# Two blocks' values per run, attention transposes two steps behind, norm factors in the weights, and VectorE making every low weight part

## The chip, the cores and the metric

The kernel runs on one core of a Trainium2 chip. Its engines are TensorE (PE, with its weight loads shown as PEld), VectorE (DVE), ScalarE (ACT), GpSimd (POOL) and the queue of SyncE (SP) that issues most transfers. The metric is device time in microseconds (us) for one launch. Before the change it is 1147.07 us, the median of three runs from 1146.75 to 1149.39 us.

## The reference

One encoder layer over 1024 tokens of width 1024, with 16 learned meta tokens in front, all in float32:

```
u = rmsnorm(h, norm_g)                       # h: 16 meta tokens + 1024 tokens
z = u @ w_in                                 # one projection, split by columns
gq gk gv r_f r_b g_gate  nq nk nv n_gate = split(z)

# group A: gated linear attention, 4 heads, both directions, chunked scan
o_gla = rmsnorm(o_f + o_b, gla_out_norm_g) * silu(g_gate)

# group B: neighbourhood attention, 16 heads of 64, on a 16 x 64 grid
qn, kn = rmsnorm(nq, q_norm_g), rmsnorm(nk, k_norm_g)
s   = qn . kn / 8 + rpb (8 x 16 window)  ++  qn . km / 8 + meta_bias
o_na = softmax(s) . (v window ++ v meta) * silu(n_gate)

out = h + concat(o_gla, o_na) @ w_out        # the 16 meta tokens are dropped
```

Here `rmsnorm(x, g)` is x times 1/sqrt(mean(x^2) + 1e-6) times g. The factor `norm_g` multiplies each of the 1024 input columns of the projection, so it can as well multiply the rows of `w_in`: (x * g) @ w equals x @ (g * w). The factor 1/sqrt of a token is applied after the projection, in both kernels.

## The kernel before

**Split products.** A float32 product is made of three TensorE matmuls. Each operand is split into a high part in TensorE's rounded float format (`wh`, `uh`) and the remainder (`wl`, `ul`); `mm3` (L414 to L416) multiplies high by high, high by low and low by high into one PSUM bank. These dense matmuls of the projection are nearly all of TensorE's work. The token side, `uh` and `ul`, is made once, at the start, per block of 128 tokens (`u_part` for the first two blocks, `u_split` for the other six). The weight side comes in pieces of 128 rows by up to 512 columns: `piece_dma` loads one into `raw`, and `piece_split` makes `wh` and `wl` from it when a slot of nine comes free (`release`, `pump`). Three pairings of engines are used there: ACT for `wh` with POOL for `wl` (63 pieces), DVE for both (24 pieces), and ACT with DVE (63 pieces, once the linear attention has begun). The tables `SPLIT_ACT` and `NA1_ACT` choose between the first two.

**Two interleaved programs.** `Sched` records the program in an order written out at build time. A filler (`fill_na`, later `fill_gla`) gives the dense matmuls in small steps; a main generator gives the attention. `S.run` lets the main generator place its own TensorE work and, between (`gap`, `to`), as much filler as it asks for; `need` runs filler until a named result is due. `S.defer(ns, fn)` places other engines' work a number of estimated nanoseconds later. Every engine then executes its own list strictly in that order and waits on semaphores. So TensorE always has dense work to do, unless an instruction at the head of its list waits.

**Neighbourhood attention, pair by pair.** Eight pairs of heads run through `attn(p)`. Each pair has eight query blocks u (128 queries each). For pair p the projection tiles (`dense_na`) give `nat` (queries and keys) and `vnat` (values); `k_prep` transposes the keys on TensorE (`kmt`, `kt`) into `K1`, `K2`; `q_prep` transposes two blocks of queries (`qt`). A step s does this, on two heads a = 0, 1:

- `transposes` of block s-1: the normalised probabilities P are transposed into the PSUM banks `pp` (L829, 6 matmuls), and copied into `PT` by ACT for a = 0 and DVE for a = 1;
- `softmax(s)`: the scores (`qk`, L767 and L768, into banks `s`), row maximum and bias on DVE (L795), exponential on ACT (L801, L802), and, deferred, `norm` (L815 to L818) on DVE, which divides P by its sum;
- filler for half a step;
- `pv` of block s-1: six matmuls (L848) of `PT` with the values, into one bank `po` whose two halves of 64 rows hold the two heads; the trace has two records for each of these matmuls. After blocks 3 and 7 DVE multiplies `po` into the gate `ng` (L858);
- filler for the other half.

There are 9 steps for 8 blocks: the ninth holds the transposes and values of block 7 alone. Then `attn(p+1)` starts with `need` and `k_prep`. The third chunk of values of blocks 0 and 7 is `kvm`, the 16 meta tokens, the only chunk with 16 rows.

**PSUM.** Eight banks: `pd` 2 (dense), `ps` 2 (scores, and at the start `junk` and `rb`), `pp` 2 (transposes), `po` 1, `pt` 1.

**The start.** `u_rstd` squares a block's rows on ACT, into a bank `junk` that nothing reads, and POOL makes `rs`, the 1/sqrt factor of each token. For the transposed outputs the factors of a block must stand along the free axis, in all partitions (`rbc`): `u_diag` makes a diagonal matrix `dg` on DVE (L376), and `u_spread` multiplies it with a matrix of ones on TensorE (`rb`, L381) and copies the result. The table `START_AT` gives the place of each such step in pair 0's dense work.

**Later.** `wd_prep` (L1018 to L1024) prepares the decay weights, for pairs 2 and 4, 20 us after those pairs' start in the scheduler's count. From about 630 us on the linear attention runs, then the output projection (`pout`), without neighbourhood attention.

## Time and profile before

| | |
|---|---|
| median of three runs | 1147.07 us |
| the profiled execution's own time | 1147.51 us |
| its span, first to last instruction | 1145.7 us |
| TensorE busy | 1122.2 us, 98% |
| VectorE, ScalarE, GpSimd busy | 769.9, 533.5, 300.7 us |
| mean granted TensorE clock | 0.998 |

The profile page gives busy time per engine and per group of instructions; the groups' last column is the idle time of the engine just before them, with what ended it. Matmuls overlap in their pipeline and a "busy" TensorE need not be streaming at its pace: two dense matmuls in a row start a fixed time apart, and whatever one start is later than that is lost, whether or not the page shows it as idle. So the timeline of starts is read here beside the idle column. The stages: start to about 60 us, one pair of heads for each 68 to 69 us until about 541 us, the end of neighbourhood attention and the first linear attention weights to about 630 us, then linear attention and output projection.

### The profile page before, as it was taken

To read this page: it belongs to the slowest core of one execution; us is meant where nothing else is said; L and a number is where in the kernel's file an instruction comes from. 1 tells how busy PE (TensorE), PEld (TensorE's weight loads), DVE (VectorE), ACT (ScalarE), POOL (GpSimd) and SP (SyncE) were. 2 spreads that over 40 slices of the span, in tenths; PEclk is the share of its full clock that TensorE was granted. 3 is DMA by queue.
4 is the path that set the end of the run, shared out by engine and by line. 5 is a ranking of instruction groups with operands and counts; after the bars stand their busy time and mean duration, and the time that the engine had idled before them with its cause. 6 is when DMAs were issued, how large, how long until landed. Compare 5 with 4: busy or idle time off the path is not lost.

```text
span 1145.7 us, 18925 instructions
## 1 busy us (share of the span) xinstructions
PE 1122.2 (98%) x6739; PEld 976.7 (85%) x6739; DVE 769.9 (67%) x1963; ACT 533.5 (47%) x1379; POOL 300.7 (26%) x415
## 2 busy tenths in 40 slices
PE   8899999999999999999999999999999999999998
PEld 7789898888988889898889789889978978888886
DVE  6867777777677776777665775675486578656352
ACT  6756565664655656565454541542343254313120
POOL 4753535336253443634221101001101000000000
PEclk9999999999999999999999999999999999999999
DMA  8720402203030030401223513512612375314132
GB/s 259 225 75 2 128 2 73 63 2 128 1 109 27 10 120 1 128 2 32 76 57 102 165 28 84 153 36 79 170 42 66 93 206 166 120 42 130 50 115 102
DMA packets 74277, 99.34 MB, mean 87 GB/s; under 512 B 6532, under 2 KB 45188, under 8 KB 74184
## 3 DMA queue, kind: packets, MB, share of 16 engines
q1 hardware_dynamic: 69960, 89.76, 26.0%
q0 software_dynamic: 4224, 8.39, 2.5%
q8 instruction: 53, 0.87, 0.3%
q14 instruction: 40, 0.33, 0.1%
HBM read 72.89 MB, written 21.04 MB: 82 GB/s over the span
## 4 chain that ended last, share of the span: by engine, by line
PE 79%; DVE 7%; issue 5%; POOL 3%; ACT 3%; DMA 2%; SPq 0%; POOLq 0%; DVEq 0%; ACTq 0%
PE pn_na L414 6%; PE pn_na L416 5%; PE pn_na L415 5%; PE pout L414 5%; PE pout L416 5%; PE pout L415 5%; PE po L848 3%; PE pp L829 3%; PE pz_gz L414 3%; PE pz_gz L415 3%; PE pz_gz L416 3%; PE pz_gg L414 2%; PE pn_gv L414 2%; PE pz_gg L416 2%; PE pz_gg L415 2%
## 5 line engine op out<-in xcount | busy, mean ns | idle before, releaser
L414 PE MATMUL pn_na<-wh,uh 128*128 128x384 f32 x512 | 179.7, 351 | 1.5 <-ACT wh L257 1.0
L415 PE MATMUL pn_na<-wl,uh 128*128 128x384 f32 x512 | 173.5, 339 | 1.7 <-POOL wl L258 1.4
L416 PE MATMUL pn_na<-wh,ul 128*128 128x384 f32 x512 | 173.0, 338 | 0.1
L212 POOL TENSOR_SCALAR post<-post 128x1 f32<-128x1 f32 x32 | 6.8, 213 | 378.4 <-ACT on L1219 378.4
L414 PEld LDWEIGHTS pn_na<-wh,uh 128*128 128x128 f32 x512 | 96.4, 188 | 10.0 <-issue 7.8
L414 PE MATMUL pout<-wh,oh 128*128 128x512 f32 x256 | 103.3, 404 | 0.2 <-DVE acc L1343 0.2
L416 PE MATMUL pout<-wh,oh 128*128 128x512 f32 x256 | 101.4, 396 | 0.0
L415 PE MATMUL pout<-wl,oh 128*128 128x512 f32 x256 | 101.4, 396 | 0.0
L415 PEld LDWEIGHTS pn_na<-wl,uh 128*128 128x128 f32 x512 | 96.6, 189 | 4.1 <-POOL wl L258 3.0
L416 PEld LDWEIGHTS pn_na<-wh,ul 128*128 128x128 f32 x512 | 96.4, 188 | 0.8 <-DVE ul L361 0.7
L258 POOL TENSOR_TENSOR wl<-raw,wh 128x512 fp32r<-128x512 f32 (+2 forms) x63 | 83.2, 1337 | 45.0 <-PE pn_gv L415 27.7
L1343 DVE TENSOR_TENSOR acc<-acc,pout 128x512 f32<-128x512 f32 x64 | 43.9, 685 | 66.8 <-PE pout L416 66.8
L801 ACT ACTIVATE P<-P,sm 128x384 f32<-128x384 f32 x96 | 58.4, 609 | 56.2 <-DVE sm L798 56.2
L414 PE MATMUL pn_gv<-wh,uh 128*128 128x256 f32 (+1 forms) x256 | 75.3, 294 | 0.0
L416 PE MATMUL pn_gv<-wh,ul 128*128 128x256 f32 (+1 forms) x256 | 72.8, 285 | 0.0
L415 PE MATMUL pn_gv<-wl,uh 128*128 128x256 f32 (+1 forms) x256 | 72.8, 284 | 0.0
L795 DVE CUSTOM_DVE_ANT_0 P<-s,wt 128x416 f32<-128x416 f32 (+1 forms) x128 | 69.6, 544 | 2.3 <-PE s L768 2.2
L213 POOL TENSOR_TENSOR ss<-ss,epsm 128x4 f32<-128x4 f32 x64 | 69.0, 1078 | 5.3
L818 DVE TENSOR_SCALAR P<-P,sm 128x384 f32<-128x384 f32 (+1 forms) x128 | 66.9, 523 | 4.5
L254 ACT ACTIVATE wh<-raw 128x512 fp32r<-128x512 f32 x63 | 39.5, 630 | 48.7 <-PE pz_gz L415 20.4
L835 DVE COPY PT<-pp 128x384 f32<-128x384 f32 (+1 forms) x80 | 36.3, 470 | 33.5 <-PE pp L829 33.0
L416 PEld LDWEIGHTS pout<-wh,oh 128*128 128x128 f32 x256 | 48.3, 189 | 11.6
(361 smaller groups left out, 2969.4 us busy)
## 6 DMA issues: line engine op xcount, KB each, us to landing
raw<-in_w_na_dram SPq DMA_DIRECT2D x56, 256.0 KB, 2.8
v_scr<-gvst SPq DMA_DIRECT2D x64, 128.0 KB, 2.3
raw<-in_w_o_dram SPq DMA_DIRECT2D x32, 256.0 KB, 3.2
oin<-o_scr SPq DMA_DIRECT2D x32, 256.0 KB, 3.1
v<-v_scr POOLq DMA_DIRECT2D x4, 1536.0 KB, 9.4
VM<-vnat SPq DMA_DIRECT2D x8, 512.0 KB, 4.5
o_scr<-ng SPq DMA_DIRECT2D x8, 512.0 KB, 3.5
raw<-in_w_gz_dram SPq DMA_DIRECT2D x16, 256.0 KB, 2.8
```

What stands on the lines that cost most here:

```text
L213: pool.tensor_tensor(dst, dst, epsm[: dst.shape[0], :eng_n], OP.pow)
L254: act.activation(wh[:, :n], r[:, :n], AF.Copy)
L258: pool.tensor_tensor(wl[:, :n], r[:, :n], f32(wh[:, :n]), OP.subtract)
L414: pe.matmul(ps, ah, bh, start=start, stop=False)
L415: pe.matmul(ps, ah, bl, start=False, stop=False)
L416: pe.matmul(ps, al, bh, start=False, stop=stop)
L795: dve.tensor_tensor_reduce(P[:, :n], ps[:, :n], wt[2 * p + a][:, off : off + n], 1.0, -3.0e38, OP.add, OP.max, mx)
L801: act.activation(loc, loc, AF.Exp, bias=mx, accum_out=sm[:, a : a + 1])
L818: dve.tensor_scalar(loc, loc, r, None, OP.mult)
L829: pe.transpose(pp[:w, c * 128 : c * 128 + 128], Ps[a][0][:, c0 : c0 + w], ident)
L835: dve.tensor_copy(t[:w, e0:e1], pp[:w, e0:e1])
L1343: dve.tensor_tensor(a, a, ps, OP.add)
```

## The change

1. **Attention (`attn` becomes `attn_all`).** One generator for all pairs. The transposes of a block now come two steps after its scores instead of one (`wait` holds up to two blocks, `turn` transposes one). Transposed blocks collect in `done`, and `gather` does their value products: at steps 3, 5 and 7, two blocks each time, in one run. Blocks 6 and 7 are finished after the next pair's `need`: a `turn`, 2000 ns of filler, a `turn`, 700 ns, the next pair's `k_prep`, 800 ns, and one `gather` (`TAIL_NS`). The buffers of `P` go from 4 to 6 and of `sm` from 2 to 3. The second load of the values (`vload`) is due by step 3 instead of 1.
2. **Norm factors.** `norm_g` no longer multiplies the tokens: `u_part` copies, `u_split` and `u_meta` lose a DVE multiplication. `piece_split` multiplies each weight row by its factor instead, as the scale of ACT's copy and as the first operation of DVE's.
3. **Weight split.** Every `wh` is made by ACT, every `wl` by DVE; POOL makes none, DVE makes no `wh`. A piece that packs two or four row blocks takes two or four instructions on each engine, since each has its own factor. The output projection's pieces stay as they were.
4. **Start.** `u_rstd` squares in place instead of into a PSUM bank. `u_diag` is gone: `u_spread` uses the column of factors, broadcast along its free axis, as the stationary operand and the identity as the moving one.
5. **Small moves.** The static copies into `K2` and `Q2` go from DVE to ACT, `wd_prep` makes its high part on ACT and reads it directly.

```diff
@@ piece_split
-            if gpool[0] is not None:
+            if key[0] == "o":
                 act.activation(wh[:, :n], r[:, :n], AF.Copy)
                 dve.tensor_tensor(wl[:, :n], r[:, :n], f32(wh[:, :n]), OP.subtract)
-            elif (NA1_ACT[j - 8] if 8 <= j < 16 else SPLIT_ACT[key[0]][j % 4]):
-                act.activation(wh[:, :n], r[:, :n], AF.Copy)
-                pool.tensor_tensor(wl[:, :n], r[:, :n], f32(wh[:, :n]), OP.subtract)
-            else:
-                dve.tensor_copy(wh[:, :n], r[:, :n])
-                dve.tensor_tensor(wl[:, :n], r[:, :n], f32(wh[:, :n]), OP.subtract)
+            for t in range(pack if key[0] != "o" else 0):
+                ts = slice(t * (n // pack), (t + 1) * (n // pack))
+                g = gT[:, pack * i + t : pack * i + t + 1]
+                act.activation(wh[:, ts], r[:, ts], AF.Copy, scale=g)
+                dve.scalar_tensor_tensor(wl[:, ts], r[:, ts], g, f32(wh[:, ts]), OP.mult, OP.subtract)
@@ u_part, u_split
-        g = gT[:, k : k + 1]
-        act.activation(uh[:, k, ts], xk, AF.Copy, scale=g)
-        dve.scalar_tensor_tensor(ul[:, k, ts], xk, g, f32(uh[:, k, ts]), OP.mult, OP.subtract)
+        act.activation(uh[:, k, ts], xk, AF.Copy)
+        dve.tensor_tensor(ul[:, k, ts], xk, f32(uh[:, k, ts]), OP.subtract)
...
-        for ks in halves:
-            dve.tensor_tensor(x3[:, ks], x3[:, ks], gT[:, ks, None].to_broadcast([128, 4, 128]), OP.mult)
@@ u_rstd, u_diag, u_spread
-            junk = ps_tile("ps", f"junk{b}_{i}", 2)
-            act.activation(junk, xr[b][:, 512 * i : 512 * i + 512], AF.Square, accum_out=st[:, i : i + 1])
+            half = xr[b][:, 512 * i : 512 * i + 512]
+            act.activation(half, half, AF.Square, accum_out=st[:, i : i + 1])
...
-    def u_diag(b):
-        dg[b] = nap.tile([128, 128], F32, tag="dg", name=f"dg{b}", bufs=3)
-        dve.tensor_scalar(dg[b], ident, rs[:, b : b + 1], None, OP.mult)
...
-        pe.matmul(ps[:, 0:128], ones, dg[b], start=True, stop=True)
+        pe.matmul(ps[:, 0:128], rs[:, b : b + 1].to_broadcast([128, 128]), ident, start=True, stop=True)
@@ attn becomes attn_all (softmax, transposes and pv are otherwise as before)
-        for s in range(9):
-            PT = None
-            if prev is not None:
-                PT = transposes(*prev)
-                pu = prev[0]
+        def turn():
+            p, u, *rest = wait.pop(0)
+            done.append((p, u, transposes(p, u, *rest)))
+
+        def gather():
+            while done:
+                pv(*done.pop(0))
+
+        for p in range(NPAIR + 1):
+            if p < NPAIR:
+                yield ("need", ("nat", p))
+            if wait:
+                turn()
                 yield ("w", 654)
-            if s < 8:
-                prev = (s, *softmax(s))
+                yield ("gap", TAIL_NS[0])
+                turn()
+                yield ("w", 654)
+                yield ("gap", TAIL_NS[1])
+            if p < NPAIR:
+                yield from k_prep(p)
+            if done:
+                yield ("gap", TAIL_NS[2])
+                gather()
+                yield ("w", 1420)
...
+            yield ("gap", ATTN_NS - (TAIL_NS[2] + 1420.0 if p else 0.0))
...
+            for s in range(8):
+                if len(wait) == 2:
+                    turn()
+                    yield ("w", 654)
+                wait.append((p, s, *softmax(p, s)))
...
-            else:
-                yield ("gap", LAST_NS)
-            if PT is not None:
-                if s == 1:
-                    for m in vload:
-                        m()
-                pv(pu, PT)
-                yield ("w", 710)
+                if s % 2 and s > 1:
+                    if s == 3:
+                        for m in vload:
+                            m()
+                    gather()
+                    yield ("w", 1420)
@@ wd_prep
-        dve.tensor_copy(w[0:98], st[0:98, 0:512])
-        act.activation(st[64:98, 512:1024], f32(w[64:98]), AF.Copy)
-        dve.tensor_tensor(w[64:96], st[64:96, 0:512], st[64:96, 512:1024], OP.subtract)
+        act.activation(w[0:98], st[0:98], AF.Copy)
+        dve.tensor_tensor(w[64:96], st[64:96], f32(w[64:96]), OP.subtract)
```

The number of TensorE instructions is the same; their order is not. The first place is a value product in the middle of pair 1, on TensorE. In the names, `pn` is a dense tile, `PT120` the transposed probabilities of pair 1, block 2, head 0, and `vnat1`, `VM` are its values. Before:

```order
L416 MATMUL pn_na2_3_1962<-wh21_1547,ul_85 128x384
L848 MATMUL po10_1840<-PT120_1970,vnat1_883 64x128
L848 MATMUL po10_1840<-PT121_1976,vnat1_883 64x128
...
L848 MATMUL po10_1840<-PT120_1970,VM_99 64x128
L848 MATMUL po10_1840<-PT121_1976,VM_99 64x128
L414 MATMUL pn_na2_3_1962<-wh22_1573,uh_84 128x384
```

Now, at step 7, blocks 4 and 5 in one run:

```order
L401 MATMUL pn_na2_7_2223<-wh20_1474,ul_85 128x384
L824 MATMUL po14_2286<-PT140_2164,vnat1_838 64x128
L824 MATMUL po14_2286<-PT141_2170,vnat1_838 64x128
...
L824 MATMUL po14_2286<-PT141_2170,VM_99 64x128
L824 MATMUL po14_2286<-PT150_2246,vnat1_838 64x128
...
L824 MATMUL po14_2286<-PT151_2252,VM_99 64x128
L399 MATMUL pn_na2_7_2223<-wh21_1481,uh_84 128x384
```

Twelve matmuls stand where six stood. In the whole list 64 runs of six become 32 runs of twelve. Of the 64, 57 returned to dense work and 7 ran straight into the next pair's `kmt`; all 32 return to dense work.

The second place is the change from pair 1 to pair 2, on TensorE, where `pz` is the dense gate tile. Now:

```order
L805 MATMUL pp160_2377<-ident_76,P160_2176 128x128 x3
L805 MATMUL pp161_2383<-ident_76,P161_2184 128x128 x3
...
L805 MATMUL pp170_2403<-ident_76,P170_2258 128x128 x2
L805 MATMUL pp170_2403<-ident_76,P170_2258 16x128
L805 MATMUL pp171_2410<-ident_76,P171_2265 128x128 x2
L805 MATMUL pp171_2410<-ident_76,P171_2265 16x128
...
L673 MATMUL kmt2_2423<-ident_76,kvm2_1842 128x16
L679 MATMUL kt2_0_2426<-ident_76,nat2_0_1694 128x128
...
L824 MATMUL po14_2286<-PT160_2381,vnat1_838 64x128
L824 MATMUL po14_2286<-PT161_2387,vnat1_838 64x128
```

Before, block 6's transposes stood with block 7's scores, and the values of block 7 came directly ahead of `kmt2`. Now two transposes stand alone, six dense matmuls lie between the second of them and `kmt2`, and the keys' banks `kt` are the two `pp` banks just used. The values of both blocks follow the keys.

The third place is the start, on VectorE, where `x_103` is token block 0 and `wl_179` the fourth weight piece. Before:

```order
L349 SCALAR_TENSOR_TENSOR ul<-x_103,gT,uh 128x128 x4
L260 CAST wh_178<-raw_113 128x384
L261 TENSOR_TENSOR wl_179<-raw_113,wh_178 128x384
L349 SCALAR_TENSOR_TENSOR ul<-x_115,gT,uh 128x128 x3
L349 SCALAR_TENSOR_TENSOR ul<-x_103,gT,uh 128x128
```

Now:

```order
L343 TENSOR_TENSOR ul<-x_103,uh 128x128
L256 SCALAR_TENSOR_TENSOR wl_146<-raw_106,gT,wh_145 128x384
L343 TENSOR_TENSOR ul<-x_103,uh 128x128
L256 SCALAR_TENSOR_TENSOR wl_157<-raw_108,gT,wh_156 128x384
L343 TENSOR_TENSOR ul<-x_103,uh 128x128
L256 SCALAR_TENSOR_TENSOR wl_168<-raw_110,gT,wh_167 128x384
```

VectorE now makes the low part of each weight piece between the low parts of the tokens; the first three used to be GpSimd's.

More of the change, by code (lines that the diff above doesn't have):

```diff
@@ L591, in at @@
                 ("load", x_load), ("split", u_split), ("rows", x_rows), ("rstd", u_rstd),
[L592 removed]
+                ("evac", lambda t: tile_evac(banks.pop(t), t)), ("spread", u_spread),
             ):
@@ new lines, with softmax, norm @@
+    po = {}
+    def softmax(p, u):
+        n = span(u)[1]
+        off = 144 if u == 0 else 0
+        sm = nap.tile([128, 8], F32, tag="sm", name=f"sm{p}{u}", bufs=3)
+        Ps, norms = [], []
+        Q1["rest"]()
+        for a in range(2):
+            ps = qk(p, u, a)
+            P = nap.tile([128, 432], F32, tag="P", name=f"P{p}{u}{a}", bufs=6)
+            mx = sm[:, 4 + a : 5 + a]
+            dve.tensor_tensor_reduce(
+                P[:, :n], ps[:, :n], wt[2 * p + a][:, off : off + n], 1.0, -3.0e38, OP.add, OP.max, mx
+            )
+            dve.tensor_scalar(mx, mx, -1.0, None, OP.mult)
+            if n == 416:
+                loc, met = P.rearrange("p (b t) -> p b t", t=BLK)[:, :, 0:128], P[:, 128:144]
+                act.activation(loc, loc, AF.Exp, bias=mx, accum_out=sm[:, a : a + 1])
+                act.activation(P[:, 295:416:8], met, AF.Exp, bias=mx, accum_out=sm[:, 2 + a : 3 + a])
+            else:
+                loc = P[:, :n]
+                act.activation(loc, loc, AF.Exp, bias=mx, accum_out=sm[:, a : a + 1])
+            Ps.append((P, loc))
+        if u % 2 == SILU_STEP:
+            run_silu()
+        def norm(a):
+            s = sm[:, a : a + 1]
+            r = sm[:, 6 + a : 7 + a]
+            if n == 416:
+                dve.tensor_tensor(s, s, sm[:, 2 + a : 3 + a], OP.add)
+            dve.reciprocal(r, s)
+            loc = Ps[a][1]
+            dve.tensor_scalar(loc, loc, r, None, OP.mult)
+        return Ps, [S.defer(NORM_NS[0], lambda: norm(0)), S.defer(NORM_NS[1], lambda: norm(1))]
@@ new lines, in transposes @@
+    def transposes(p, u, Ps, norm):
+        ch = ((0, 128), (144, 128), (128, 16) if u in (0, 7) else (288, 128))
+        PT = []
+        for a in range(2):
+            norm[a]()
+            pp = ps_tile("pp", f"pp{p}{u}{a}", 2)
+            for c, (c0, w) in enumerate(ch):
+                pe.transpose(pp[:w, c * 128 : c * 128 + 128], Ps[a][0][:, c0 : c0 + w], ident)
+            t = nap.tile([128, 384], F32, tag="PT", name=f"PT{p}{u}{a}", bufs=4)
+            for w, e0, e1 in ((128, 0, 256), (16, 256, 384)) if u in (0, 7) else ((128, 0, 384),):
+                if a == 0:
+                    act.activation(t[:w, e0:e1], pp[:w, e0:e1], AF.Copy)
+                else:
+                    dve.tensor_copy(t[:w, e0:e1], pp[:w, e0:e1])
+            PT.append(t)
+        return PT
@@ new lines, in pv @@
+    def pv(p, u, PT):
+        u4 = u % 4
+        if u4 == 0:
+            po[0] = ps_tile("po", f"po{p}{u}", 1)
+        b0 = span(u)[0]
+        vals = [vnat[p][:, b0], vnat[p][:, b0 + 1], kvm[p][:, 128:256] if u in (0, 7) else VM[:, b0 + 2]]
+        for c, V in enumerate(vals):
+            w = V.shape[0]
+            for a in range(2):
+                pe.matmul(
+                    po[0][64 * a : 64 * a + 64, u4 * 128 : u4 * 128 + 128],
+                    V[:, 64 * a : 64 * a + 64],
+                    PT[a][:w, c * 128 : c * 128 + 128],
+                    start=c == 0, stop=c == 2,
+                )
+        if u4 == 3:
+            finish(gate_rest)
+            g = zt[("ng", p)]
+            gv = g.rearrange("p (r i c) -> p i r c", r=16, i=8, c=8)[:, u - 3 : u + 1]
+            dve.tensor_tensor(gv, po[0].rearrange("p (i r c) -> p i r c", i=4, r=16, c=8), gv, OP.mult)
+            if u == 7:
+                sp.dma_start(o_scr[8 + p], g)
@@ new lines, in attn_all @@
+    def attn_all():
+        wait, done = [], []
+        def turn():
[9 more added lines that the diff above has]
+                turn()
+                yield ("w", 654)
+                yield ("gap", TAIL_NS[0])
[8 more added lines that the diff above has]
+                yield ("w", 1420)
+            if p == NPAIR:
+                break
+            vload = v_load(p)
+            if p in WD_AT:
+                wd_load(WD_AT.index(p))
+                S.defer(WD_NS, lambda d=WD_AT.index(p): wd_prep(d))
+            if p == NPAIR - 2:
+                r_static()
+            yield ("gap", ATTN_NS - (TAIL_NS[2] + 1420.0 if p else 0.0))
+            f0 = S.fill
+            f1 = (p + 1) * (NAT_NS + GATE_NS) + (NAT_NS if p < 7 else GLA_NS - 9000.0)
+            for s in range(8):
[3 more added lines that the diff above has]
+                wait.append((p, s, *softmax(p, s)))
@@ L1356 @@
     S.filler = fill_na()
-    for p in range(NPAIR):
-        if p in WD_AT:
-            wd_load(WD_AT.index(p))
-            S.defer(WD_NS, lambda d=WD_AT.index(p): wd_prep(d))
-        if p == NPAIR - 2:
-            r_static()
-        S.run(attn(p))
+    S.run(attn_all())
     S.until(("gv", 0))
```

111 lines of the change are left out of this document (11 added, 100 removed).

## The prediction

> **What bounds the kernel now.** I read the page first, then the timeline of TensorE's starts.
>
> ```profile
> span 1145.7 us, 18925 instructions
> PE 1122.2 (98%) x6739; PEld 976.7 (85%) x6739; DVE 769.9 (67%) x1963; ACT 533.5 (47%) x1379; POOL 300.7 (26%) x415
> ```
>
> TensorE is busy 98% of the span, and the change removes none of its matmuls. What is left to win is 23.5 us of idle time (1145.7 - 1122.2) and starts that are late without being called idle. The second kind shows in the starts around one value product of pair 3 (start, duration, instruction):
>
> ```profile
> 301.67 0.34 PE L415 MATMUL pn_na<-wl,uh 128*128 128x384 f32 x1
> 301.84 0.34 PE L416 MATMUL pn_na<-wh,ul 128*128 128x384 f32 x1
> 302.11 0.66 PE L848 MATMUL po<-PT,vnat 128*64 128x128 f32 x8
> 302.60 0.39 PE L848 MATMUL po<-PT,VM 128*64 128x128 f32 x4
> 302.91 0.44 PE L414 MATMUL pn_na<-wh,uh 128*128 128x384 f32 x1
> 303.19 0.34 PE L415 MATMUL pn_na<-wl,uh 128*128 128x384 f32 x1
> 303.37 0.34 PE L416 MATMUL pn_na<-wh,ul 128*128 128x384 f32 x1
> ...
> 304.60 0.82 PE L829 MATMUL pp<-ident,P 128*128 128x128 f32 x6
> 305.18 0.44 PE L767 MATMUL s<-K,Q 128*128 128x416 f32 x1
> ```
>
> Dense 384-column matmuls start 0.17 to 0.18 us apart (301.67, 301.84; 303.19, 303.37; I use 0.173). The last before the run is followed after 0.27 (0.10 late). The run's eight records take 0.49, 0.061 each; its last four take 0.31 instead of 0.245 (0.066 late). The first dense one after it is followed after 0.28 (0.107 late). So each run of values costs 0.27 us beside its own work, and there are 64 runs.
>
> **Part 1a, half as many runs.** 57 runs return to dense work, 7 to the next keys:
>
> ```profile
> 128.14 0.40 PE L416 MATMUL pz_na<-uh,wl 128*128 128x512 f32 x1
> 128.47 0.66 PE L848 MATMUL po<-PT,vnat 128*64 128x128 f32 x8
> 129.05 0.43 PE L848 MATMUL po<-PT,kvm 16*64 16x128 f32 x4
> 129.42 0.23 PE L690 MATMUL kmt<-ident,kvm 16*128 16x16 f32 x1
> ```
>
> Here the meta chunk starts 0.58 after the eight (0.09 late, a change to 16 rows), and `kmt` 0.37 after it (0.125 late). The change leaves 32 runs, all to dense work: 25 x 0.27 = 6.8 us go, and 7 x (0.10 + 0.125) = 1.6. Inside a merged run only block 0's meta chunk is followed by a 128-row chunk, so 8 x 0.09 = 0.7 may come, of which some is only moved. Net **-7.9**. Bounds: 0, if lateness belonged to each block rather than to each run, and -8.4. I take -7.9, since it is read at the run's two ends and not between the eight and the four. The transposes cost no entry and the same exit whether scores or dense work follows, and there are 64 of them in either order.
>
> **Part 1b, the attention's own waits.** Groups with idle time and its cause, then three examples:
>
> ```profile
> L829 PE MATMUL pp<-ident,P 128*128 128x128 f32 (+1 forms) x384 | 53.7, 273 | 3.1 <-DVE P L818 3.1
> L848 PE MATMUL po<-PT,vnat 128*64 128x128 f32 x512 | 43.0, 286 | 2.2 <-DVE PT L835 2.2
> L381 PE MATMUL rb<-dg,ones 128*128 128x128 f32 x16 | 3.6, 308 | 3.9 <-DVE dg L376 3.1 <-ACT junk L368 0.9
> ...
> 470.10 0.49 PE L829 MATMUL pp<-ident,P 128*128 128x128 f32 x3
> 471.28 0.52 PE L829 MATMUL pp<-ident,P 128*128 128x128 f32 x3 [0.69 <-DVE P L818]
> ...
> 223.59 0.43 PE L848 MATMUL po<-PT,vnat 128*64 128x128 f32 x2
> 225.15 0.54 PE L848 MATMUL po<-PT,vnat 128*64 128x128 f32 x5 [1.12 <-DVE PT L835]
> ...
> 222.40 0.63 ACT L1022 ACTIVATE wdst<-wd 34x512 f32<-34x512 f32 x1 [2.75 <-DVE wd L1021]
> ...
> 55.26 0.41 PE L416 MATMUL pz_na<-uh,wl 128*128 128x512 f32 x1
> 57.90 0.46 PE L381 MATMUL rb<-dg,ones 128*128 128x128 f32 x2 [2.23 <-DVE dg L376]
> ```
>
> Three transposes take 0.29 (half of 304.60 to 305.18); at 470.10 they take 1.18, because the second head's P is not yet normalised. That costs 0.89 for 0.69 shown idle, so 3.1 us shown are 4.0 lost. With a whole step of dense work more between a block's scores and its transposes, that wait cannot stay. The waits for `PT` are two of 1.12 us, one in each pair where `wd_prep` holds ACT 2.75 us and DVE behind it; each loses 1.4. After the change the older block's six matmuls (0.73 us) run first and that chain is shorter. Together 6.8; I take **-6.0**. Bounds: 0, if other waits step in, and -6.8.
>
> **Part 4, the start's `rb`.** At 57.90 TensorE waits for `dg`, which stood deep in DVE's list. Now only the factor from POOL is needed, made well before; the bank is no longer shared with `junk`. 3.9 us shown plus restarts; two of the three examples' causes go with certainty. **-4.2**, bounds -2.2 (the `dg` waits merely move to POOL's factor in one case) and -4.6.
>
> **Parts 2 and 3, the weights and the first 25 us.**
>
> ```profile
> 6.45 2.12 POOL L258 TENSOR_TENSOR wl<-raw,wh 128x384 fp32r<-128x384 f32 x2 [5.33 <-ACT wh L257]
> ...
> 10.04 0.56 DVE L261 TENSOR_TENSOR wl<-raw,wh 128x384 fp32r<-128x384 f32 x1
> ...
> 10.71 1.23 DVE L349 SCALAR_TENSOR_TENSOR ul<-x,gT,uh 128x128 fp32r<-128x128 f32 x4
> ...
> 10.28 1.28 ACT L348 ACTIVATE uh<-x,gT 128x128 fp32r<-128x128 f32 x4 [1.78 <-DMA x<-in_xt_dram]
> ...
> 6.42 0.44 PE L414 MATMUL pn_na<-wh,uh 128*128 128x384 f32 x1 [1.00 <-ACT wh L257]
> 7.50 0.44 PE L415 MATMUL pn_na<-wl,uh 128*128 128x384 f32 x1 [0.64 <-POOL wl L258]
> ...
> 16.44 0.44 PE L415 MATMUL pn_na<-wl,uh 128*128 128x384 f32 x1
> ...
> 23.91 0.44 PE L414 MATMUL pn_na<-wh,uh 128*128 128x384 f32 x1 [0.35 <-ACT uh L359]
> ```
>
> POOL takes about 1.03 us for a low part (2.12 for two), DVE alone 0.56, and a token's low part about 0.3 (1.23 for four), so a piece takes DVE 0.86. The first matmul still waits for the same load, at 6.42; its low part comes at about 7.0 instead of 7.50, and the three after it gain a little more each; then the second token block, which lands at 10.28 as before, holds everybody; so most of the early gain is lost there. By the eighth piece (16.44) I estimate 1.0 us gained, six to eight differences of 0.17 between 1.03 and 0.86. The multiplication that `u_split` loses stood ahead of ACT's `uh`, and at 23.91 TensorE waits for that: 0.35 shown idle, about 0.8 with the restart and the low part behind it. **-1.8**, bounds 0 and -4.
>
> Later DVE gets 63 low parts more and loses 24 casts:
>
> ```profile
> core 0: us, PE busy (x) PEld busy (x) DVE busy (x) ACT busy (x) POOL busy (x), PEclk, DMA share, GB/s
> 197.00:266.00 69.00, 67.01 (x439) 59.60 (x436) 50.45 (x150) 40.84 (x116) 28.23 (x37) 1.00 0.16 51
> L255 DVE TENSOR_TENSOR wl<-raw,wh 128x512 fp32r<-128x512 f32 x63 | 43.1, 689 | 21.6 <-ACT wh L254 20.4 <-PE pk L1168 0.5 <-PE pa L1249 0.2
> L261 DVE TENSOR_TENSOR wl<-raw,wh 128x512 fp32r<-128x512 f32 x20 | 22.6, 1130 | 0.7
> L260 DVE CAST wh<-raw 128x512 fp32r<-128x512 f32 x20 | 10.1, 503 | 1.1 <-DMA raw<-in_w_gz_dram 0.9
> L1114 DVE SCALAR_TENSOR_TENSOR ga<-ga,gk 128x1024 f32<-128x1024 f32 x8 | 9.8, 1219 | 0.0
> L1116 DVE TENSOR_TENSOR gm<-gm,gq 128x1024 f32<-128x1024 f32 x8 | 9.8, 1220 | 0.0
> ```
>
> Per pair: six low parts come at 0.69 (L255, while POOL is quiet), 4.1 us; two casts go, 1.0; and the two it already made shrink from 1.13 (L261, beside POOL's) towards 0.69, 0.9. So 2.2 us more on 50.45 of 69: 76%, hidden under dense work. Without that cover it would be 2.2 x 7 = 15 us. The packed pieces cost one more fixed part per extra instruction; 384 columns at 0.56 and 512 at 0.69 give about 0.17 for it, under 6 us over 300 and more, hidden too. ACT gets 24 more `wh` on 47% busy. [...]
>
> That the new instruction (multiply, then subtract) runs as fast as a subtraction rests on the last two rows: 1219 against 1220 ns for 1024 columns.
>
> **New waits.** The last transposes of a pair now stand 1.4 us (six dense 512-column matmuls, 0.173 x 512 / 384 = 0.23 each) before `kt`, which reuses their banks. The trace before has no case of a bank reused so soon; between 0 and 0.5 us may be waited for the copies at each of 7 pair changes, and I charge 0.2. Behind a late copy would queue ACT's key copies and so the first scores, but these come 7 us later. With ACT and DVE orders that are new everywhere, I charge **+1.8** in all; bounds 0 and +8.
>
> **Sum.** -7.9 - 6.0 - 4.2 - 1.8 + 1.8 = -18.1. The profiled execution's own time is 1147.51, within 0.44 of the median of the runs: 1147.5 - 18.1 = 1129.4, 1129.0 on the scale of the median. I say **1129**.
>
> **Rivals.**
>
> *Only the runs count.* The waits of 1b and 4 and the start are replaced by others, since DVE's list is as full as before: 1147.1 - 7.9 = 1139. For it: DVE is the releaser in nearly all these waits and gets more work. Against: at each of them the waiting instruction now stands later or its producer is gone.
>
> *The lateness belongs to blocks.* 1a gives nothing: 1137. Against it, the even 0.061 inside a run.
>
> [...]
>
> *Slower: the pair change clogs DVE.* Six more low parts fall into the same few microseconds as the last norms, the last copies of `PT` and the query's and key's remainders, in one strict list. If TensorE waited for all six at each of 7 pair changes, 4.1 x 7 = 28.7 us come, 1b's gain goes, and the time is 1147.1 - 13.9 + 28.7 = 1162. It decides the sign from 13.9 / 7 = 2.0 us per pair change. Against it: the 1b waits found no such delay, and by the scheduler's count the keys now start some 4 us later after the last dense tile than before.
>
> *The change doesn't do what it says* is excluded for the order: TensorE's list has 32 runs of twelve.
>
> **Chances.** Forecast 0.70 (its own range 1121 to 1135), only the runs 0.16, blocks 0.04, half pace 0.04, slower 0.06. The range must keep the second, and the lower end the full bounds of the start and the waits: 1120 to 1140. A measurement can tell about 0.3%, 3.4 us. Faster than that 0.91, within it 0.03 (the upper end of the second rival with some new waits), slower 0.06.
>
> **What will show it.** Right: the runs of values start 0.10 late and end 0.17 late, 32 times; no idle time before `pp` and `po` on DVE; `rb` without a wait; L415 at about 7.0 first. Wrong: idle time of TensorE before `kt` or before a dense matmul on DVE's low part, 0.5 us or more at each pair change; a low part of 512 columns at over 1 us; an interval inside a merged run that is late at the border of its two blocks.

## The result, and the profile after

The changed kernel takes 1156.49 us (median of four runs, 1155.55 to 1160.21) against 1147.37 for the kernel before on the same chip: a ratio of 1.0083, 95% interval 1.0057 to 1.0108. It is 9 us slower, where 18 us faster was forecast. Its profiled execution took 1156.79 us. In what follows, times from other chips are compared by their ratio to the kernel before, and 0.001 is 1.15 us.

The page's head of the changed kernel, and its groups of TensorE instructions (line, instruction, count | busy us, mean ns | idle us just before, and what ended it):

```profile
span 1154.7 us, 18967 instructions
PE 1116.4 (97%) x6739; PEld 977.1 (85%) x6739; DVE 767.6 (66%) x2023; ACT 563.4 (49%) x1459; POOL 219.8 (19%) x352
...
L805 PE MATMUL pp<-ident,P 128*128 128x128 f32 (+1 forms) x384 | 52.5, 272 | 0.6 <-DVE sm L790 0.6
L750 PE MATMUL s<-K,Q 128*128 128x416 f32 (+1 forms) x128 | 48.0, 379 | 13.4 <-DVE Q L724 13.0
L824 PE MATMUL po<-PT,vnat 128*64 128x128 f32 x512 | 41.0, 281 | 0.0
L457 PE MATMUL pm_na<-wh,um 128*48 128x256 f32 x64 | 15.5, 281 | 9.4 <-DVE Q L724 8.6 <-DVE um L392 0.8
L367 PE MATMUL rb<-ident,rs 128*128 128x128 f32 x16 | 3.3, 287 | 1.0 <-ACT rbc L368 1.0
```

The groups of the scores and of `pm_na`, the projection of the meta tokens, in the kernel before:

```profile
L767 PE MATMUL s<-K,Q 128*128 128x416 f32 (+1 forms) x128 | 47.7, 377 | 0.0
L472 PE MATMUL pm_na<-wh,um 128*48 128x256 f32 x64 | 15.6, 283 | 1.1 <-DVE um L407 1.1
```

TensorE's busy time fell by 5.8 us and the span rose by 9.0, so its idle time rose from 23.5 to 38.3. The old waits are gone: `pp` 3.1 to 0.6, `po` 2.2 to 0, `rb` 3.9 to 1.0. In their place stand two waits that the kernel before did not have, both for VectorE's `Q` (L724): 13.0 us at the scores `s`, and 8.6 at `pm_na`.

The merged runs look as forecast. TensorE's timeline around one of them (start, duration, instruction):

```profile
100.19 0.34 PE L401 MATMUL pn_na<-wh,ul 128*128 128x384 f32 x1
100.46 0.66 PE L824 MATMUL po<-PT,vnat 128*64 128x128 f32 x8
100.94 0.39 PE L824 MATMUL po<-PT,VM 128*64 128x128 f32 x4
101.16 0.61 PE L824 MATMUL po<-PT,vnat 128*64 128x128 f32 x8
101.60 0.39 PE L824 MATMUL po<-PT,VM 128*64 128x128 f32 x4
101.92 0.44 PE L399 MATMUL pn_na<-wh,uh 128*128 128x384 f32 x1
102.20 0.34 PE L400 MATMUL pn_na<-wl,uh 128*128 128x384 f32 x1
```

The entry takes 0.27 (0.10 late), the border of the two blocks 0.22 (0.055 each, not late), the exit 0.32 and 0.28 (0.07 and 0.11 late).

**Where the time came from.** For every TensorE start that comes over 0.2 us later than the usual interval for its pair of shapes (the median over all the traces here), I add up the lateness. That gives 25.9 us before and 43.4 after: +17.5, less 8 for 32 runs saved, so 9.5 where the spans differ by 9.0. The choice of the limit moves this by a few us (without one it is 113.5 and 129.2), so it is a rough account. The start up to pair 0's keys (`kmt`) is shorter, 53.7 against 60.9 us. Each of the first seven pairs then takes 71.6 us on average instead of 69.2.

**Wait 1, a bank held longer than planned.** Four pieces of the changed kernel's timeline in pair 3, of TensorE, ScalarE and VectorE:

```profile
286.18 0.38 PE L711 MATMUL qt<-ident,nat 128*128 128x128 f32 x2
...
288.90 1.04 ACT L635 ACTIVATE sig<-ng 128x1024 f32<-128x1024 f32 x1
289.85 0.77 ACT L717 ACTIVATE Q<-qt 64x256 fp32r<-64x256 f32 x2
...
290.65 0.86 DVE L724 TENSOR_TENSOR Q<-qt,Q 64x256 fp32r<-64x256 f32 x2 [0.74 <-ACT Q L717]
...
289.88 0.34 PE L401 MATMUL pn_na<-wh,ul 128*128 128x384 f32 x1
291.66 0.29 PE L457 MATMUL pm_na<-wh,um 128*48 128x256 f32 x1 [1.44 <-DVE Q L724]
```

`qt` and `pm_na` share the one bank `pt`. The scheduler's estimate holds it `Q_NS + 2000` = 3420 ns for `qt`; in fact VectorE lets go of it 5.3 us later (286.18 to 291.51), because ScalarE's copy stands behind four exponentials and the gate's. 1.6 us are lost in each of six pairs. In the kernel before, `pm_na` came a step later and never met that:

```profile
284.89 0.38 PE L728 MATMUL qt<-ident,nat 128*128 128x128 f32 x2
...
295.35 0.32 PE L472 MATMUL pm_na<-wh,um 128*48 128x256 f32 x1
```

**Wait 2, a VectorE product stretched beside GpSimd.** GpSimd, VectorE, ScalarE and TensorE in pair 3, from the same timeline:

```profile
307.54 2.40 POOL L639 TENSOR_TENSOR ng<-ng,sig 128x1024 f32<-128x1024 f32 x1
...
307.60 2.62 DVE L545 TENSOR_TENSOR nat<-nat,ss 128x256 f32<-128x256 f32 x1 [0.89 <-POOL ss L209]
...
310.95 0.62 ACT L776 ACTIVATE P<-P,sm 128x384 f32<-128x384 f32 x1 [5.04 <-DVE sm L773]
...
319.35 0.43 PE L750 MATMUL s<-K,Q 128*128 128x416 f32 x1 [1.04 <-DVE Q L724]
```

`nat`'s normalisation, 0.42 us elsewhere, takes 2.61 to 2.62 us in each of six pairs, where it starts 0.06 us after the gate's multiplication on GpSimd (2.40 us) and ends 0.28 after it. Row maxima, exponentials and `Q` come late one behind the other, and step 6 waits for `Q`: 1.3 us lost, six times. In the kernel before, the same GpSimd instruction ran beside VectorE instructions that did not stretch; the row maximum, which reads one operand from PSUM, took its usual 0.58:

```profile
304.51 2.40 POOL L656 TENSOR_TENSOR ng<-ng,sig 128x1024 f32<-128x1024 f32 x1
...
306.08 0.58 DVE L795 CUSTOM_DVE_ANT_0 P<-s,wt 128x416 f32<-128x416 f32 x1
```

The stretching itself is older than the change. In the kernel before, `nat`'s normalisation took 1.5 us thirteen times, each time beside GpSimd's low part of a weight at the change of pairs, and TensorE's `kt` waited for it 0.2 us at most. What is new is the place.

**Wait 3, the decay weights.** In pairs 2 and 4 `wd_prep` now has its high part on ScalarE. ScalarE, VectorE and TensorE of the changed kernel in pair 2:

```profile
230.92 0.63 ACT L1031 ACTIVATE wd<-wdst 98x512 fp32r<-98x512 f32 x1
...
231.58 0.68 DVE L1032 TENSOR_TENSOR wd<-wdst,wd 32x512 fp32r<-32x512 f32 x1 [2.87 <-ACT wd L1031]
...
234.73 0.87 DVE L724 TENSOR_TENSOR Q<-qt,Q 64x256 fp32r<-64x256 f32 x2
...
235.30 0.43 PE L750 MATMUL s<-K,Q 128*128 128x416 f32 x1 [3.18 <-DVE Q L724]
```

VectorE's list stands 2.87 us behind ScalarE's instruction, with the norms and `Q` queued behind it; TensorE waits 3.18 us for the scores.

### The profile page after: what moved, and what is told of

Its sections match the earlier page's. It is cut to its first block, busy times and chain, and to the rows that moved or that the text cites. A ratio compares the mean times of both kernels' runs of the same rounds, so it can differ in the third digit from the quotient of the medians.

```text
span 1154.7 us, 18967 instructions
## 1 busy us (share of the span) xinstructions
PE 1116.4 (97%) x6739; PEld 977.1 (85%) x6739; DVE 767.6 (66%) x2023; ACT 563.4 (49%) x1459; POOL 219.8 (19%) x352
## 5 line engine op out<-in xcount | busy, mean ns | idle before, releaser
L256 DVE SCALAR_TENSOR_TENSOR wl<-raw,gT,wh 128x256 fp32r<-128x256 f32 (+4 forms) x168 | 91.5, 582 | 38.1 <-ACT wh L255 37.1
L255 ACT ACTIVATE wh<-raw,gT 128x256 fp32r<-128x256 f32 (+4 forms) x168 | 88.0, 575 | 30.4 <-PE pz_gz L400 17.8
L793 DVE TENSOR_SCALAR P<-P,sm 128x384 f32<-128x384 f32 (+1 forms) x128 | 59.2, 462 | 4.5
L750 PE MATMUL s<-K,Q 128*128 128x416 f32 (+1 forms) x128 | 48.0, 379 | 13.4 <-DVE Q L724 13.0
```

The source lines that it names most:

```text
L255: act.activation(wh[:, ts], r[:, ts], AF.Copy, scale=g)
L256: dve.scalar_tensor_tensor(wl[:, ts], r[:, ts], g, f32(wh[:, ts]), OP.mult, OP.subtract)
L750: pe.matmul(ps[:, :n], q1[:, qs], k1, start=True, stop=False)
L793: dve.tensor_scalar(loc, loc, r, None, OP.mult)
```

## The experiments

### Which half of the change makes the waits (e1, e2)

The change was cut in two. In e1 the kernel before gets `attn_all` and all that belongs to it; in e2 it gets the rest.

```diff
@@ e1: the kernel before, plus
+TAIL_NS = (2000.0, 700.0, 800.0)
+    def attn_all():
...
+    S.run(attn_all())
@@ e2: the kernel before, plus
+                act.activation(wh[:, ts], r[:, ts], AF.Copy, scale=g)
+                dve.scalar_tensor_tensor(wl[:, ts], r[:, ts], g, f32(wh[:, ts]), OP.mult, OP.subtract)
...
```

> The kernel before with the attention part of the change alone (two blocks' values per run, one block more ahead, the two low parts of wd from the new code), while the norm factors stay in u and the weights' low parts stay spread over ScalarE, VectorE and GpSimd. Theory A: the new waits of the attention (pm_na for the meta projection's bank, s at step 6, s at step 4 of pairs 2 and 4, together about 30 us against 9.4 before) come with the new order of the attention itself, so this kernel keeps them: 1147.4 - 8 (runs) + 20 (waits) = 1159 us, 1155 to 1163. Rival B: they come from VectorE being loaded with all low weight parts, so without that load they are mostly gone: 1147.4 - 8 - 6 = 1133 us, below 1142.

> The kernel before with all the rest of the change (norm factors multiplied into the weights, all low weight parts on VectorE, the start without diag), and the attention as it was. Theory A (waits come with the attention's new order): the start's late starts fall by 4.8 us as in the changed kernel and the attention stays as before: 1142.5 us, 1140 to 1146. Rival B (VectorE's added load makes the waits): the attention's waits of 20 us come here too: 1162 us, above 1152.

Measured: e1 1157.6 us, ratio 1.0089 (1.0072 to 1.0107); e2 1152.0, 1.0041 (1.0029 to 1.0054). In e1 all three waits are there, `pm_na` 1.44 us idle six times and `s` 3.19 us at 239.95: they belong to the attention's new order (with the new `wd_prep`, which e1 has too), as theory A says. e2 came out between both theories. Its start is 5.9 us shorter (`kmt` at 55.0 against 60.9), and all of it is lost again in the attention (pair 7's `kmt` at 545.6 against 545.5), because the old attention's waits for VectorE's norms grow. The group of transposes in e2, beside 3.1 us in the kernel before:

```profile
L812 PE MATMUL pp<-ident,P 128*128 128x128 f32 (+1 forms) x384 | 54.8, 274 | 9.2 <-DVE P L801 9.2
```

From pair 7's keys to the end of TensorE's last matmul it takes 4.8 us more than before (601.0 against 596.2): 1.5 us up to the last values, 1.3 in a longer wait for VectorE's `RS` (2.7 against 1.4), and some 2 behind that wait. A lower clock could account for these 2, as an estimate: behind e13's wait for `RS` (2.67 us) it was 0.58 from 611 to 615 us, and dense matmuls of 512 columns started 0.43 us apart instead of 0.23. The longer waits for VectorE fit added low parts that were not hidden; no run separates these from the rest of e2's half.

### The three waits, each taken away at its cause (e3 to e6)

```diff
@@ wait 1 (e3, e4)
-        pt = pt_tile(f"qt{p}_{i}", 3100 if i == 0 else Q_NS + 2000)
+        pt = pt_tile(f"qt{p}_{i}", 3100 if i == 0 else Q_NS + 4500)
@@ wait 2 (e3, e5)
-            S.defer(ns[2], lambda: (pool if gpool[0] is None else dve).tensor_tensor(g, g, e, OP.mult)),
+            S.defer(ns[2], lambda: dve.tensor_tensor(g, g, e, OP.mult)),
@@ wait 3 (e3, e6)
-        dve.tensor_tensor(w[64:96], st[64:96], f32(w[64:96]), OP.subtract)
-        dve.scalar_tensor_tensor(w[96:98], f32(w[96:98]), ident[96:98, 97:98], st[96:98], OP.mult, OP.subtract)
+        def low():
+            dve.tensor_tensor(w[64:96], st[64:96], f32(w[64:96]), OP.subtract)
+            dve.scalar_tensor_tensor(w[96:98], f32(w[96:98]), ident[96:98, 97:98], st[96:98], OP.mult, OP.subtract)
+        S.defer(6000.0, low)
```

> The changed kernel with the three new waits each taken away at its cause: the bank of the Q transposes is planned as held 4500 ns instead of 2000 ns beyond Q's own delay, so that the meta projection comes a tile later; the gate's last multiplication runs on VectorE instead of GpSimd; VectorE's two low parts of wd come 6000 ns after ScalarE's part. Theory C (three separate causes that add up): 11 + 8 + 6 = 25 us go, 1156.5 - 25 = 1131.5 us, 1128 to 1137. Rival D (one lateness of VectorE and ScalarE that shows at whatever wait comes first, so that a removed wait comes back at the next): not below 1148 us.

> The changed kernel with the first of the three edits alone: the bank of the Q transposes planned as held 4500 ns instead of 2000 ns beyond Q's own delay. Theory C: the seven waits of pm_na behind VectorE's Q (1.43 us idle, 1.59 us lost each) go and nothing else: 1156.5 - 11 = 1145.5 us, 1143 to 1149. Rival D: the same lateness is waited for at s or at the next bank: 1153 us or more.

> The changed kernel with one edit: the gate's last multiplication (128x1024, 2.40 us on GpSimd) runs on VectorE. Theory P (while GpSimd works on two SBUF inputs, a VectorE instruction on two SBUF inputs stands still): the normalisation of nat beside it falls from 2.62 us to 0.42 us, VectorE pays 1.2 us for the multiplication itself elsewhere, and the six waits of s at step 6 (1.28 us lost each) go: 1156.5 - 8 = 1148.5 us, 1146 to 1152. Rival V (VectorE is simply full there, whatever GpSimd does): nat stays long or another instruction takes its place, VectorE has 1.2 us more a pair, and the time does not fall: 1155 to 1162 us.

> The changed kernel with one edit: VectorE's two low parts of wd come 6000 ns after ScalarE's part, in pairs 2 and 4 alone. If VectorE's stand behind ScalarE is the cause of the two long waits of s at step 4 (3.18 and 3.14 us idle, with the slow matmuls behind them some 6 us together): 1156.5 - 6 = 1150.5 us, 1149 to 1153, and those waits fall to those of the other pairs. Rival (the steps 4 of these pairs wait for something else): 1156 us.

| kernel | median us | ratio to before (95%) | against the changed kernel |
|---|---|---|---|
| e4, wait 1 alone | 1152.6 | 1.0048 (1.0029 to 1.0066) | -0.0035, -4.0 us |
| e5, wait 2 alone | 1151.1 | 1.0015 (1.0005 to 1.0024) | -0.0068, -7.8 us |
| e6, wait 3 alone | 1154.0 | 1.0035 (1.0022 to 1.0048) | -0.0048, -5.5 us |
| e3, all three | 1139.3 | 0.9928 (0.9909 to 0.9947) | -0.0155, -17.8 us |

The last column is the difference of two ratios, each uncertain by about 0.003. By it e5 and e6 did what theory and price said (the median of e6 lies over its range in us, on a chip where the kernel before takes 1149.4). In e5 `nat` never stretches, and the multiplication costs VectorE 1.22 us a piece; groups of VectorE instructions in e5, beside 39.8 us and 622 ns in the changed kernel:

```profile
L545 DVE TENSOR_TENSOR nat<-nat,ss 128x256 f32<-128x256 f32 x64 | 26.8, 418 | 5.5 <-POOL ss L209 5.2
L639 DVE TENSOR_TENSOR ng<-ng,sig 128x1024 f32<-128x1024 f32 x8 | 9.7, 1218 | 0.1
```

The single edits add up to 17.3 of e3's 17.8 us, but e4 shows that this is no proof of three separate causes. The waits of `pm_na` went (six, not the seven that the expectation counted: 9.5 us), and only 4.0 were won: with the tiles in a new order another VectorE instruction met GpSimd's multiplication, just where `wd` was. Timeline of VectorE, GpSimd and TensorE in e4:

```profile
230.22 2.29 DVE L790 TENSOR_TENSOR sm<-sm 128x1 f32<-128x1 f32 x1
...
230.11 2.39 POOL L639 TENSOR_TENSOR ng<-ng,sig 128x1024 f32<-128x1024 f32 x1
...
227.42 0.82 PE L805 MATMUL pp<-ident,P 128*128 128x128 f32 x6
234.61 0.68 PE L750 MATMUL s<-K,Q 128*128 128x416 f32 x1 [6.37 <-DVE Q L724]
```

A sum of two columns, 0.16 us elsewhere, took 2.29 us, and the wait for `Q` in pair 2 doubled to 6.37 us. e3 missed its 1131.5 by 8 us: the first `s` of step 4 still waits 1.1 to 1.3 us in most pairs (8.2 us idle at `s` in all), so rival D holds in part.

### The rest of the lateness: moved, then removed (e7, e9 to e14)

e7 is e3 with the transposes of the queries a step earlier; e9 puts the merged runs of e7 later in their steps; e10 is e1 with the three edits, e11 is e10 with e7's and e9's edits.

```diff
@@ e7 (on e3), and in e9, e11, e13, e14
-                if s % 2 == 1 and s < 7:
+                if s % 2 == 0 and s < 6:
@@ e9 (on e7) and e11
-PV_AT = (0.5, 0.5, 0.5, 0.6, 0.5, 0.5, 0.5, 0.5)
+PV_AT = (0.5, 0.5, 0.5, 0.8, 0.5, 0.8, 0.5, 0.8)
```

> The kernel of e3 (1139.3 us) with the next two blocks' Q transposes one step earlier (behind steps 0, 2 and 4 instead of 1, 3 and 5). In e3 the first s of a step 4 still waits for VectorE's Q, 1.1 to 1.3 us idle in seven pairs, and that of step 6 0.36 us in three; the trace shows why: ScalarE takes Q out of the bank only behind the four exponentials of the step (297.4 us against the transposes at 292.2). Theory Q (with a step more, Q is there in time): 1139.3 - 9 = 1130 us, 1128 to 1134. Rival E (Q's copies now stand ahead of the exponentials, whose P is then late for the transposes at pp): no gain, 1138 us or more.

> The kernel of e7 with the merged PV runs later in their steps (0.8 of the step's weight work ahead of them instead of 0.6 and 0.5, in steps 3, 5 and 7). In e7 the waits of s for Q were gone (the steps from pp to s 11.9 us shorter) and came back inside the merged run: po waits for VectorE's PT, 0.34 us idle in four pairs and 1.70 us in two, with slow matmuls behind them, 10.2 us together, because VectorE does P's normalisation and Q ahead of that copy. Theory (the copy is only some 1.1 us late, and 0.3 of a step is about 2 us): the waits at po go and none takes their place: a ratio to the kernel before of 0.986, 1132 us, 1128 to 1136. Rival D (the lateness of VectorE moves on to the next wait again): 0.9925, 1138 us or more.

> The kernel of e1 (the attention part of the change alone, 1157.6 us) with the three edits of e3. It tells what the other half of the change (norm factors in the weights, low parts on VectorE) is worth once the three waits are gone. By the pair of kernels with the waits (e1 1157.6, the changed kernel 1156.5) it is worth -1.1 us: this kernel would take 1139.3 + 1 = 1140.5 us, 1138 to 1143. By the pair with the old attention (the kernel before 1147.4, e2 1152) it costs 4.3 us: this kernel would take 1135 us, 1132 to 1137.5.

> The kernel of e10 with both further edits, Q's transposes a step earlier and the merged runs later, a candidate for the fastest. If the waits of VectorE's list are what keeps e10 up, as in e3, and VectorE is freer here (the low parts of the weights are shared with GpSimd): e10 minus 8 us, 1127 to 1133 us. If not, as e10 within 3 us.

Measured: e7 0.9925 (0.9908 to 0.9941), e9 0.9921 (0.9896 to 0.9947), e10 0.9924 (0.9903 to 0.9944), e11 0.9921 (0.9898 to 0.9944), all as e3's 0.9928. The expected gains did not come: the wait only changed its place. In e7 `s` waits no longer, and `po` waits for VectorE's copy of `PT`. VectorE, GpSimd and TensorE in e7's pair 1:

```profile
160.33 1.22 DVE L639 TENSOR_TENSOR ng<-ng,sig 128x1024 f32<-128x1024 f32 x1
...
166.82 0.86 DVE L724 TENSOR_TENSOR Q<-qt,Q 64x256 fp32r<-64x256 f32 x2
168.16 0.56 DVE L811 COPY PT<-pp 128x384 f32<-128x384 f32 x1
...
160.38 2.03 POOL L209 TENSOR_TENSOR ss<-ss,epsm 128x4 f32<-128x4 f32 x1
...
163.48 0.81 PE L805 MATMUL pp<-ident,P 128*128 128x128 f32 x6
168.78 0.54 PE L824 MATMUL po<-PT,vnat 128*64 128x128 f32 x5 [0.34 <-DVE PT L811]
```

The transposes are done by 164.3; VectorE copies them at 168.16, after the norms, `Q` and a sum. In e9 that wait shrank (`po` 5.3 us idle to 1.4) and `pz_na` began to wait for ScalarE's `vnat` (4.0 us). e10 decided the two estimates of the weights' half in favour of the first: with the new attention it is worth about nothing (e3 0.9928, e10 0.9924).

Two ways out were then told apart: take work from VectorE (e12 on e3, e13 on e7), or cut up the one long instruction (e14 on e7).

```diff
@@ e12, e13
-                if a == 0:
-                    act.activation(t[:w, e0:e1], pp[:w, e0:e1], AF.Copy)
-                else:
-                    dve.tensor_copy(t[:w, e0:e1], pp[:w, e0:e1])
+                act.activation(t[:w, e0:e1], pp[:w, e0:e1], AF.Copy)
@@ e14
-            S.defer(ns[2], lambda: dve.tensor_tensor(g, g, e, OP.mult)),
+            *(S.defer(ns[2] + 1500.0 * t, lambda c=slice(256 * t, 256 * t + 256): dve.tensor_tensor(g[:, c], g[:, c], e[:, c], OP.mult)) for t in range(4)),
```

> The kernel of e3 with both copies of P's transposes out of their bank on ScalarE (before: one on ScalarE, 0.49 us, one on VectorE, 0.56 us). VectorE has 64 copies of 0.56 us, 36 us in all, less. Theory L (VectorE's list is what is late at the waits of s for Q): the waits of 1.1 to 1.3 us at step 4 shrink by about 0.6 us each and no others come: a ratio to the kernel before of 0.988, 1135 us, 1132 to 1138. Theory A (ScalarE is as full there: Q's own copy on ScalarE comes behind the exponentials and now behind one copy more): 0.993, 1139 us or more.

> The kernel of e7 (Q a step earlier) with both copies of P's transposes on ScalarE. In e7 the merged run waited for VectorE's copy, 10 us in all with the slow matmuls behind; ScalarE's copy of the other half stood 0.7 us earlier (ended 167.9 us against VectorE's 168.7). Theory L: the waits at po go, 0.985, 1131 us, 1128 to 1135. Theory A: ScalarE's copies are late in the same way, 0.991 to 0.994, 1138 us or more.

> The kernel of e7 with the gate's last multiplication on VectorE (1.22 us in one piece, GpSimd's power beside it 2.03 us instead of 1.01) in four pieces of 256 columns, 1500 ns apart. Theory G (the one long instruction and the power it stretches hold up the row maxima by some 2 us, and PT by as much): the waits at po for PT shrink to under 0.2 us in the five pairs without wd, 0.988, 1134 us, 1131 to 1138. Otherwise: 0.9925, 1139 us or more, with VectorE's sum the same.

Measured: e12 1136.0 us, 0.9879 (0.9864 to 0.9894); e13 1129.6 us, 0.9819 (0.9804 to 0.9834); e14 1138.6 us, 0.9888 (0.9866 to 0.9911), which overlaps e7's interval. e13 answers it: with the copy on ScalarE, which had room, no other wait takes the place of the old one. In e14 the waits for `PT` did not shrink: 0.46 us in the four pairs without `wd` (0.34 in e7), because two of the four pieces now stand ahead of the copy, and 1.9 in the two pairs with it (1.7 in e7). So theory G is false in its mechanism, although the ratio is the one it gave; the trace, which is of e14's slowest run, does not show where a gain would come from. One of these waits, in e14's pair 1:

```profile
171.30 0.54 PE L824 MATMUL po<-PT,vnat 128*64 128x128 f32 x5 [0.47 <-DVE PT L811]
```

e13 has the answering lines:

```profile
span 1126.2 us, 19039 instructions
PE 1109.6 (99%) x6739; PEld 979.6 (87%) x6739; DVE 731.2 (65%) x1951; ACT 586.2 (52%) x1539; POOL 206.9 (18%) x344
...
L805 PE MATMUL pp<-ident,P 128*128 128x128 f32 (+1 forms) x384 | 52.5, 272 | 0.1
L750 PE MATMUL s<-K,Q 128*128 128x416 f32 (+1 forms) x128 | 46.4, 367 | 0.0
L821 PE MATMUL po<-PT,vnat 128*64 128x128 f32 x512 | 42.8, 282 | 0.0
L457 PE MATMUL pm_na<-wh,um 128*48 128x256 f32 x64 | 15.3, 278 | 0.7 <-DVE um L392 0.7
```

No wait of the attention is left after pair 0's keys, late starts add up to 16.5 us in the whole kernel, and VectorE's busy time fell by only 32 us of 764 against e7. The stretch that counts is a pair. Pair 3 of the changed kernel (first fence) and pair 2 of e13 without its last 0.5 us (second), busy time by engine:

```profile
core 0: us, PE busy (x) PEld busy (x) DVE busy (x) ACT busy (x) POOL busy (x), PEclk, DMA share, GB/s
270.80:340.90 70.10, 67.57 (x451) 60.91 (x450) 50.70 (x152) 41.97 (x117) 21.95 (x32) 1.00 0.17 53
```

```profile
192.30:258.90 66.60, 66.60 (x449) 61.33 (x449) 47.21 (x145) 45.38 (x128) 20.82 (x31) 1.00 0.18 59
```

VectorE is busy 72% of its pair in the one and 71% in the other. That share told nothing of the waits.

### What each part is worth when nothing waits (e8, e15 to e17)

e8 undoes the merging in e3, e16 in e13. e17 undoes the weights' half in e13. e15 is the kernel before with the relief of e13 (bank plan, gate on VectorE, `Q` early, both copies on ScalarE).

```diff
@@ e8, e16
-                if s % 2 and s > 1:
+                if done:
                     if s == 3:
                         for m in vload:
                             m()
                     gather()
-                    yield ("w", 1420)
+                    yield ("w", 710)
```

> The kernel of e3 (1139.3 us) with the PV matmuls of one block per run again, 64 runs of six in place of 32 of twelve, all else the same. The prediction priced the merging at 7.9 us (0.247 us a run saved): 1139.3 + 8 = 1147 us, 1145 to 1149. Rival (a run's entry and exit hide in waits that are there anyway, now that the waits are few): 1139 to 1142 us.

> The kernel before with the same relief as e13: the Q bank planned as held 4500 ns, the gate's last multiplication on VectorE, Q's transposes a step earlier, both copies of P's transposes on ScalarE (its wd left as it is). Theory (the change keeps its own worth, and the relief takes from the kernel before only its own waits at pp and po, 6 us): a ratio of 0.995, 1142 us, 1139 to 1146. Rival (the relief is all, the change has no worth of its own): 0.982 to 0.985, 1128 to 1132 us. Third (Q's new place, ScalarE's copies and the one-block pipeline get in each other's way): above 1150 us.

> The kernel of e13 with the PV matmuls of one block per run again. In e8 against e3 the seven runs in place of four cost 0.95 us a pair by the trace (0.317 us for each run more), the other 9 us of that difference were new waits. Here, with slack in VectorE: 24 runs more by 0.317 us, 7.6 us, 1129.6 + 7.6 = 1137 us (0.9885), 1135 to 1140. Rival (runs of one block again find P's transposes late, as in e8): 1143 us or more.

> The kernel of e13 with the weights' half of the change undone (norm factors in u, low parts shared with GpSimd, the old start). By e10 against e3 the weights' half is worth 0.7 us, a start 5 us shorter against later parts 4 us longer: 1129.6 + 1 = 1130.5 us (0.983), 1128 to 1133. Rival (with VectorE relieved its later cost is gone, and the start's gain stays): 1134 us or more.

| kernel | ratio to before (95%) | difference | what it is the price of |
|---|---|---|---|
| e15 | 0.9970 (0.9958 to 0.9982) | e13 - e15: -0.0151 | the whole change: 17.3 us faster |
| e16 | 0.9891 (0.9872 to 0.9911) | e13 - e16: -0.0072 | merged runs: 8.3 us |
| e17 | 0.9843 (0.9828 to 0.9858) | e13 - e17: -0.0024 | weights and start: 2.8 us, barely clear of its uncertainty |

Each difference is uncertain by about 0.002 to 0.0025 (the two intervals added in squares). All three lie in their expected ranges, and the relief alone gives the kernel before only 0.3%: its transposes still wait for VectorE's norms (5.8 us idle at `pp`). e8 in contrast gave 1.0074 (1.0057 to 1.0091), 16.8 us over e3 and not 8. In pairs without other trouble seven runs in place of four cost 0.95 us. The rest is two waits of 2.2 us for ScalarE's `PT`, longer waits for `Q` (9.6 us idle in all, where e3 has 8.2), and slow matmuls behind four of these waits (behind the one that ended at 303.52, 0.32 us apart instead of 0.17). An experiment on one cost, made on a kernel that is full of waits, measures the waits too; e16 made the same edit where there were almost none (0.9 us idle at `po` in all).

## Why the prediction was wrong

- **What bounds it, the method of late starts:** right, roughly. Late starts and the 8 us of the runs give the span of the changed kernel against before to 0.5 us (17.5 - 8), and e13's to 2.1 us (16.5 - 25.9 - 8 = -17.4, against -19.5).
- **1a, half as many runs (-7.9):** right; 8.3 us in e16 (uncertain by some 3 us, and with 0.9 us of idle time at `po` in it), and the interval at the border is on time. Only in the run of blocks 0 and 1, behind the 16 rows of the meta tokens, is that border 0.15 us late: 8 x 0.15 = 1.2 us, where the prediction named 0.7 and took off 0.5 (8.4 - 7.9).
- **1b, the attention's own waits (-6.0):** right in mechanism, `pp` and `po` on VectorE are gone. The whole change less the two other parts leaves 17.3 - 8.3 - 2.8 = 6.2 us; that is a remainder, uncertain by some 4 us, not a run of its own.
- **Part 4 and parts 2 and 3 (-4.2 and -1.8):** right in their sum at the start, where pair 0's keys come 5.8 us earlier in e13 than in e17. That the sum fits so well is in part luck: `rb` still waits 1.0 us, for ScalarE's copy of the factors (L368), which part 4 had at nothing, and no run measures the two terms apart. Wrong in "hidden": 2.1 us of it are given back later by the spans of e13 and e17, and in the old attention more than all of it (e2).
- **Half pace (0.04 in the chances), a new low part at twice the subtraction's time:** false. A low part of 512 columns takes 747 ns on average in the changed kernel (56 of them), where the subtraction alone took 689 before; three in a row take 2.07 us.
- **New waits (+1.8, bounds 0 and +8): the step that failed.** Between the changed kernel and e13, the same change without its waits, lie 0.0264, 30 us; the two groups of new waits alone stand idle 21.6 us (13.0 and 8.6). I looked for new waits at the pair change alone, where two early `kt` wait 1.6 us in all and none later. The order on VectorE and ScalarE inside steps 1 to 6 was not gone through: which instruction now lets go of `pt`, what stands behind ScalarE's exponentials, what runs on GpSimd at that moment. The rival on the other side priced the wrong place.
- **VectorE beside GpSimd:** the prediction had 1.13 us for a low part beside GpSimd's and 0.69 while GpSimd is quiet (means of L261 and L255), and used this for the price of VectorE's low parts alone. What GpSimd's multiplication of 2.40 us would meet in the new order was not asked. In pair 3 it started at 307.54, VectorE's product at 307.60, and that took 2.62 us in place of 0.42.

Between e3 and e13 lie 12.5 us, 10.0 in the profiled spans. Most of that is in plain sight: the scores' waits stand idle 8.2 us in e3 and not at all in e13, and late starts fall from 26.1 to 16.5. What stays open is why e13 needed both edits, `Q` earlier and the copy on ScalarE: whether VectorE's list was too long in these steps, or the copy only stood in the wrong place of it, no run tells apart.

## What to carry to other kernels

When a change moves an instruction to another step, go through the lists of the other engines for that step, and write down for each shared bank and buffer who lets go of it last, and what stands ahead of that one in its list. Here a GpSimd multiplication of 2.40 us on SBUF operands held up a VectorE product of 128x256 (2.62 us in place of 0.42) and even a sum of 128x1 (2.29 in place of 0.16), both with two SBUF operands; look at what such an instruction meets in the new order, not at its own duration alone. If removing one wait makes the next one appear, take work off the engine that releases them all, and price a part of a change only in a kernel without waits.
